# One decoder layer on one core: the front of the kernel rebuilt around the conditioning vector, constant products ahead of it, two groups in plain fp32, next weights prepared early

## The chip, the cores and the metric

The kernel runs on one core of one Trainium2 chip. The time is device time in microseconds of one execution; the time before is the median of three runs. The profile is one further execution with the hardware profiler on.

## What is computed

One conditioned layer over 256 tokens of width 2048, in fp32. Only the beginning matters here:

```
mod = silu(c) @ w_ada + b_ada          # c: one vector of 2048; six parts of 2048
shift1, scale1, ... = split(mod, 6)
h   = rms_norm(x, g_norm1) * (1 + scale1) + shift1
p   = h @ w_in                         # 2048 x 12288, then retention, HGRN2, gates
```

Everything behind `p` (two recurrent branches, two output projections, a gated feed-forward of width 5632 with a short convolution, the final norm) is untouched in its arithmetic.

## The kernel before

**Products.** A weight piece arrives by DMA as `raw`. ScalarE copies it to `wh`, a float32r tile (`upper`, L169), and VectorE subtracts to get the remainder `wl` (`rest`, L174). Activations are split into hi and lo in the same way. A product is then three float32r matmuls, hi·wh, lo·wh and hi·wl: L214, L215, L218 in `mm_cols`, and L198, L199, L203 in `mm_rows`. `raw` has 12 buffers, `wh` and `wl` 4 each, so a piece is prepared only when an earlier one has been used.

**Modulation.** `x` lies transposed (`xT`, four tiles of four 128-row blocks). Block k of `h` needs a scale column and a shift column: each is a dot product of silu(c), spread over all partitions in `sc`, with 128 rows of `w_ada`. `ada_dot` does it on VectorE, as two instructions of 1024 and 1025 columns per column vector (L458), so four per block. The norm needs 1/rms per token: `norm_x` squares the four tiles of `xT` and adds on VectorE; `token_rstd` sums over partitions with a column of ones on TensorE (L335), takes the square root on ScalarE (`rq`, L344), the reciprocal on VectorE (L345), and spreads the result with the identity (L349). `times` multiplies a block of `xT` by it (L448), `modulated` applies scale and shift (L382, L384, L386) and subtracts for lo (L387).

**The front.** `constants` brings `c` as two rows on one partition and spreads it with four matmuls against one row of ones (L296); ScalarE takes the Silu out of PSUM into `sc` (L368, L374). Then blocks k = 0 and 1 are multiplied with the first four column groups of `w_in` (`FIRST = 4`, groups 0 to 3, in PSUM).

**Behind the front.** A loop visits the groups 0 to 11 in turn, and lets each catch up with the blocks that are modulated by then: `have = min(KT, 2 + int((work - LAG) / ADA_EVERY))`, where `work` counts blocks times groups. A visited group other than 0 and 1 leaves its PSUM tile to `take`: the first time ScalarE copies it (`p<-pg`, L828), later VectorE adds it (L830).

**What sets the order.** In the front, instructions that go through `pin` keep the order in which they are written, engine by engine. Behind it a scheduler at build time chooses. Either way each engine works through one fixed list: an instruction that waits holds up what stands behind it on its engine. SyncE issues the weight DMAs (L158), ScalarE's queue the small ones of the start.

Of the kernel before, what the change touches and what calls it, by code (L numbers as in the profile page):

```python
# [12 lines left out]
F32 = mybir.dt.float32  # L13
# [22 lines left out]
LAG = 1  # L36
# [21 lines left out]
class Kernel:  # L58
    def __init__(self, ctx, tc, a):
# [12 lines left out]
        self.ordered = True  # L72

# [145 lines left out]

    def mm_wide(self, ps, items, first, last, pair):  # L220
# [54 lines left out]
    def constants(self):  # L275
# [13 lines left out]
        rows = [self.blk([1, GW], name="crow") for _ in range(2)]  # L289
        for u, row in enumerate(rows):  # L290
            nc.scalar.dma_start(out=row, in_=a["c"][:, u * GW : (u + 1) * GW])
        self.small_loads(nc.scalar, ("ident", "gn1"))
        for u in range(4):
            at = slice(u * G, (u + 1) * G)
            ps = self.po()
            nc.tensor.matmul(ps, lhsT=self.ones[0:1, :], rhs=rows[u // 2][:, u % 2 * G : (u % 2 + 1) * G], start=True, stop=True)  # L296
            self.silu.append((self.sc[:, at], ps))
# [29 lines left out]
    def token_rstd(self, parts):  # L327


        nc = self.nc  # L330
        ps = self.po()[:, :NT]
        for i, z in enumerate(parts):
            for t in range(NT):

                nc.tensor.matmul(  # L335
                    ps[:, t : t + 1],
                    lhsT=z[:, t * P : (t + 1) * P],
                    rhs=self.ones[:, 0:1],
                    start=i == t == 0,
                    stop=i == len(parts) - 1,  # L340
                    skip_group_check=True,
                )
        q = self.small([P, NT], name="rq")
        nc.scalar.activation(q, ps, AF.Sqrt, bias=self.eps1, scale=1.0 / D)  # L344
# [3 lines left out]
        for t in range(NT):  # L348
            nc.tensor.matmul(ps[:, t * P : (t + 1) * P], lhsT=q[:, t : t + 1].to_broadcast([P, P]), rhs=self.ident, start=True, stop=True)  # L349
# [7 lines left out]
    def norm_x(self):  # L357
# [3 lines left out]
        parts = []  # L361
        for i, x in enumerate(self.xT):
            z = self.blk([P, 4, T], name="sq")
            if i == 0:
                self.pin(nc.vector.tensor_tensor(z, x, x, ALU.mult))
            else:
                if i < 3:
                    self.pin(nc.scalar.activation(*self.silu.pop(0), AF.Silu))  # L368
                self.pin(nc.scalar.activation(z, x, AF.Square))
            self.pin(nc.vector.tensor_tensor(z[:, :2, :], z[:, :2, :], z[:, 2:, :], ALU.add))  # L370
            self.pin(nc.vector.tensor_tensor(z[:, 0, :], z[:, 0, :], z[:, 1, :], ALU.add))
            parts.append(z[:, 0, :])
        for part in self.silu:
            self.pin(nc.scalar.activation(*part, AF.Silu))  # L374
        self.sqrt_table()
        return parts

    def modulated(self, dst, x, k, sc, sh):
# [4 lines left out]
        if k == 0:  # L383
            self.pin(self.nc.vector.tensor_scalar(h, x, sc[:, k : k + 1], sh[:, k : k + 1], ALU.mult, ALU.add))  # L384
        else:
            self.pin(act(h, x, AF.Identity, bias=sh[:, k : k + 1], scale=sc[:, k : k + 1]))  # L386
# [65 lines left out]
    def ada_dot(self, src):  # L452

        nc = self.nc
        part = self.small([P, 2], name="dot", bufs=6)
        for u, w in enumerate((GW, D + 1 - GW)):
            raw = self.load(src[:, u * GW : u * GW + w], 1, w)
            dot = self.pin(nc.vector.scalar_tensor_tensor(raw[:, 0, :], raw[:, 0, :], 1.0, self.sc[:, u * GW : u * GW + w], ALU.mult, ALU.mult, accum_out=part[:, u : u + 1]))  # L458
# [5 lines left out]
    def scale_shift(self, name, k, sc, sh, gn):  # L464
# [5 lines left out]
        self.pin(act(sc[:, kk], gn[:, kk], AF.Identity, bias=gn[:, kk], scale=sc[:, kk]))  # L470
        part = yield from self.ada_dot(self.a[name][k, 1])
# [322 lines left out]
    def run(self):  # L794
# [38 lines left out]
        ada = [ada1(k) for k in range(KT)]  # L833
        for _ in range(3):
            next(ada[0])
        rx = self.token_rstd(parts)
        rx_sb = c.tile([P, T], F32, name="rx_sb")
        ps = [self.po2(), self.po2(), self.pg(), self.pg()][:FIRST]
        for k in range(2):
            for i in range(4 if k else 1):  # L840
                if k and i == 1:
                    self.times(k, 1, rx)
                next(ada[k])
            if k == 0:
                self.times(k, 1, rx)

            ahead = 2 * k
            uppers = [self.upper(a["wa"][g][:, k : k + 1, :], 1, G) for g in range(ahead + 1)]
            rests = [self.rest(z) for z in uppers[:ahead]]
            for _ in ada[k]:  # L850
                pass
            for g in range(FIRST):
                if g >= ahead:
                    rests.append(self.rest(uppers[g] if g < len(uppers) else self.upper(a["wa"][g][:, k : k + 1, :], 1, G)))
                wh, wl = rests[g]
# [436 lines left out]
```

## Time and profile before

| what | us |
|---|---|
| median of three runs | 1511.31 (1510.82 to 1512.48) |
| the profiled execution | 1511.24 |
| its span, first to last instruction | 1509.5 |

Lines of the profile name engines PE (TensorE matmul), PEld (its weight loads), DVE (VectorE), ACT (ScalarE), SP (SyncE); a q behind a name is the engine's instruction queue. In the timeline a row has start, time, engine, line, operation, output<-inputs, shape, count, and in brackets how long the engine had been idle and what ended that. The time of a row with a count runs from the first start to the last end. Instructions of one engine overlap a little, so that the distance between two starts (the pitch) is often shorter than the time of one. fp32 products show two records each, float32r products one.

### The profile page before, as it was taken

Reading aid. Unit: us, or ns where it says so; the run is one execution under the profiler, and the core shown is the slowest. Engines: PE = TensorE matmul, PEld = TensorE weight load, DVE = VectorE, ACT = ScalarE, POOL = GpSimd, SP = SyncE. Lnnn points to the kernel's source line nnn. Section 1 sums busy time; section 2 is a strip of 40 time slices with the busy share of each in tenths; the row PEclk is TensorE's granted clock in tenths of the full one; section 3 lists DMA queues with packets and bytes.
Section 4 is the critical chain, followed back from the end, with each engine's and each line's share of the span. In section 5 each row is a group of like instructions: output and inputs, shape, how many; then the busy total and the mean of one; then the engine's idle time right before and its main releaser. Section 6 shows DMA issues by size and latency. Waiting matters only on the chain.

```text
span 1509.5 us, 22703 instructions
## 1 busy us (share of the span) xinstructions
PE 1493.7 (99%) x8466; PEld 1275.5 (84%) x8466; DVE 1211.9 (80%) x1647; ACT 841.7 (56%) x1210; POOL 4.0 (0%) x8
## 2 busy tenths in 40 slices
PE   8999999999999999999999999999999999999997
PEld 6889899888888888888888888888888888888886
DVE  7899997998999877898977778777777769455784
ACT  6745456767775644455466555555555658344342
POOL 0000000000000000000000000000000000000000
PEclk9999999999999999999999999999999999999999
DMA  9999997777887899989847777777777666667651
GB/s 373 376 347 336 321 320 257 265 248 274 281 278 262 285 302 326 318 290 361 298 132 242 229 233 230 230 231 238 229 239 231 216 193 204 197 206 212 183 171 56
DMA packets 110994, 385.71 MB, mean 256 GB/s; under 512 B 12802, under 2 KB 13346, under 8 KB 110884
## 3 DMA queue, kind: packets, MB, share of 16 engines
q1 hardware_dynamic: 110016, 383.14, 76.7%
q8 instruction: 66, 1.08, 0.3%
q10 hardware_dynamic: 868, 1.13, 0.2%
q14 instruction: 44, 0.36, 0.1%
HBM read 382.11 MB, written 2.11 MB: 255 GB/s over the span
## 4 chain that ended last, share of the span: by engine, by line
PE 93%; DVE 3%; ACT 1%; issue 1%; DMA 1%; SPq 0%; DVEq 0%; ACTq 0%
PE pg L198 13%; PE pg L203 13%; PE pg L199 13%; PE po L1125 11%; PE pg L1125 10%; PE po L1127 5%; PE pg L1127 5%; PE pg L225 4%; PE po L198 3%; PE po L203 3%; PE po L199 3%; PE pg L228 2%; DVE wl L174 1%; DVE raw L458 1%; PE po L218 1%
## 5 line engine op out<-in xcount | busy, mean ns | idle before, releaser
L174 DVE TENSOR_TENSOR wl<-raw,wh 128x1024 fp32r<-128x1024 f32 (+1 forms) x536 | 633.1, 1191 | 233.6 <-ACT wh L169 230.6
L169 ACT ACTIVATE wh<-raw 128x1024 fp32r<-128x1024 f32 (+1 forms) x536 | 547.9, 1033 | 482.5 <-PE pg L199 167.0
L458 DVE SCALAR_TENSOR_TENSOR raw<-raw,sc 128x1024 f32<-128x1024 f32 x192 | 233.8, 1222 | 0.1
L1125 PE MATMUL po<-h2T,wh 128*128 128x512 f32 x704 | 221.1, 395 | 0.0
L1125 PE MATMUL pg<-h2T,wh 128*128 128x512 f32 x688 | 216.4, 396 | 0.0
L198 PE MATMUL pg<-wh,hT 128*128 128x512 f32 x512 | 202.1, 395 | 0.9 <-DVE p L830 0.6
L199 PE MATMUL pg<-wh,hT 128*128 128x512 f32 x512 | 199.8, 390 | 0.0
L1127 PEld LDWEIGHTS po<-h2T,wl 128*128 128x128 f32 x704 | 132.3, 188 | 31.3
L1127 PEld LDWEIGHTS pg<-h2T,wl 128*128 128x128 f32 x688 | 129.2, 188 | 31.0 <-DVE wl L174 0.5
L203 PE MATMUL pg<-wl,hT 128*128 128x512 f32 x512 | 138.4, 390 | 0.1
L1127 PE MATMUL po<-h2T,wl 128*128 128x256 f32 x704 | 138.3, 278 | 0.0
L1127 PE MATMUL pg<-h2T,wl 128*128 128x256 f32 x688 | 135.3, 278 | 0.1
L198 PEld LDWEIGHTS pg<-wh,hT 128*128 128x128 f32 x512 | 96.1, 188 | 21.3 <-ACT f L579 1.0
L203 PEld LDWEIGHTS pg<-wl,hT 128*128 128x128 f32 x512 | 96.0, 188 | 20.6 <-DVE wl L174 0.4
L199 PEld LDWEIGHTS pg<-wh,hT 128*128 128x128 f32 x512 | 96.2, 188 | 19.6 <-DVE hT L387 0.3
L1125 PEld LDWEIGHTS po<-h2T,wh 128*128 128x128 f32 x704 | 107.2, 189 | 0.0
L1125 PEld LDWEIGHTS pg<-h2T,wh 128*128 128x128 f32 x688 | 104.7, 189 | 0.0
L199 PE MATMUL pg<-wh,gs 128*128 128x512 f32 x176 | 68.6, 390 | 0.0
L198 PE MATMUL pg<-wh,gs 128*128 128x512 f32 x176 | 68.5, 389 | 0.0
L198 PE MATMUL po<-wh,gs 128*128 128x512 f32 x176 | 68.5, 389 | 0.0
L199 PE MATMUL po<-wh,gs 128*128 128x512 f32 x176 | 68.5, 389 | 0.0
L225 PE MATMUL pg<-hT,wh 128*128 128x512 f32 x256 | 65.1, 396 | 0.2 <-DVE p L247 0.2
(255 smaller groups left out, 2023.3 us busy)
## 6 DMA issues: line engine op xcount, KB each, us to landing
raw<-in_wup SPq DMA_DIRECT2D x176, 512.0 KB, 4.5
raw<-in_wdown SPq DMA_DIRECT2D x88, 512.0 KB, 4.2
raw<-in_wa SPq DMA_DIRECT2D x80, 512.0 KB, 5.7
raw<-in_ada SPq DMA_DIRECT2D x64, 512.5 KB, 5.4
raw<-in_ada SPq DMA_DIRECT2D x64, 512.0 KB, 5.5
raw<-in_wab SPq DMA_DIRECT2D x64, 512.0 KB, 5.0
raw<-in_gate SPq DMA_DIRECT2D x32, 512.5 KB, 4.3
raw<-in_wk SPq DMA_DIRECT2D x32, 512.0 KB, 5.1
```

The lines of the kernel that those rows point to most:

```text
L169: self.pin(self.nc.scalar.activation(wh, raw, AF.Copy))
L174: self.last = self.nc.vector.tensor_tensor(wl, raw, wh.bitcast(F32), ALU.subtract)
L198: nc.tensor.matmul(ps[t], lhsT=act[:, hi], rhs=wh, start=first and i == 0, stop=False)
L199: nc.tensor.matmul(ps[t], lhsT=act[:, lo], rhs=wh, start=False, stop=False)
L203: nc.tensor.matmul(ps[t], lhsT=act[:, hi], rhs=wl, start=False, stop=last and i == len(items) - 1)
L218: nc.tensor.matmul(outs[j], lhsT=wl[:, cs[j]], rhs=act[:, :T], start=False, stop=last and i == len(items) - 1, skip_group_check=True)
L225: nc.tensor.matmul(ps[z], lhsT=wh[:, z * P : (z + 1) * P], rhs=act, start=first and i == 0, stop=False)
L228: nc.tensor.matmul(ps[z][:, :T], lhsT=wl[:, z * P : (z + 1) * P], rhs=act[:, :T], start=False, stop=last and i == len(items) - 1)
L458: dot = self.pin(nc.vector.scalar_tensor_tensor(raw[:, 0, :], raw[:, 0, :], 1.0, self.sc[:, u * GW : u * GW + w], ALU.mult, ALU.mult, accu ...
L1125: self.pin(nc.tensor.matmul(ps[j + z], lhsT=wh[:, cs[z]], rhs=act, start=kt == 0, stop=False, skip_group_check=bool(begun)))
L1127: nc.tensor.matmul(ps[j + z][:, :T], lhsT=wl[:, cs[z]], rhs=act[:, :T], start=False, stop=kt == KT - 1, skip_group_check=bool(begun))
```

## The change

1. `c` comes as 16 rows of 128 and, behind the identity, on ScalarE's queue. TensorE transposes it (L320 of the new file), ScalarE takes one Silu of 128x16 (`col`, L323) and loads the square-root table at once. `spread` makes the four pieces of `sc` with four 128x128 products each (`col` broadcast, against the identity, L334); ScalarE copies them out (L410, L422).
2. `idle(n)` issues n products of constant ones, which nobody reads (L242): nine at the start, one behind the transpose, two and nine in `token_rstd`.
3. The fourth tile of `xT` is squared half by ScalarE, half by VectorE, and its four parts go to TensorE unadded: the sums over partitions become 14 products (L370) in place of 8.
4. For blocks 0 and 1 the second shift dot is cut into 512 and 513 columns. The modulation starts with scale and the first part of the shift (`begun`, L891), and VectorE adds the other two (`summed`, L882).
5. For block 0, groups 0 and 1 are multiplied in plain fp32 straight from `raw` (`mm_plain`, L225): no `wh`, no `wl`. For block 1, groups 0 and 1 go through `mm_apart` (L236), all hi·wh, then lo·wh, then hi·wl.
6. The `wh` and `wl` of group 4's first two blocks are made in the pinned part (`self.early`), ahead of block 2's dots. `LAG` goes from 1 to 2.

The numbers of float32r products behind the front stay the same; VectorE has three more `take` additions (40 for 37).

```diff
-LAG = 1
+LAG = 2
@@ Kernel
+    def mm_plain(self, ps, w, h):
+        for j in range(4):
+            out = ps[j // 2][:, j % 2 * T : (j % 2 + 1) * T]
+            self.pin(self.nc.tensor.matmul(out, lhsT=w[:, j * P : (j + 1) * P], rhs=h, start=j % 2 == 0, stop=False, skip_group_check=True))
+
+    def mm_apart(self, pss, pieces, act):
...
+        for pick, cols in ((0, slice(0, T)), (0, slice(T, 2 * T)), (1, slice(0, T))):
+            for i in n:
+                for j in range(4):
...
+    def idle(self, n):
+        ps = self.pg()[0]
+        for _ in range(n):
+            self.pin(self.nc.tensor.matmul(ps[:, :P], lhsT=self.ones, rhs=self.ones, start=True, stop=True))
@@ products
-        for step in self.pieces(src[:, k0 : k0 + kts, :], kts, gain):
+        early, self.early = self.early, None
+        for step in early or self.pieces(src[:, k0 : k0 + kts, :], kts, gain):
@@ constants
-        rows = [self.blk([1, GW], name="crow") for _ in range(2)]
-        for u, row in enumerate(rows):
-            nc.scalar.dma_start(out=row, in_=a["c"][:, u * GW : (u + 1) * GW])
-        self.small_loads(nc.scalar, ("ident", "gn1"))
-        for u in range(4):
...
-            nc.tensor.matmul(ps, lhsT=self.ones[0:1, :], rhs=rows[u // 2][:, u % 2 * G : (u % 2 + 1) * G], start=True, stop=True)
+        self.small_loads(nc.scalar, ("ident",))
+        row = self.s1([KT, P], name="crow")
+        self.pin(nc.scalar.dma_start(out=row, in_=a["c"]))
+        self.small_loads(nc.scalar, ("gn1",))
+        self.idle(9)
+        ps = self.po()[:, :KT]
+        self.pin(nc.tensor.transpose(ps, row, self.ident[:KT, :KT]))
+        self.idle(1)
+        col = self.small([P, KT], name="col", bufs=1)
+        self.pin(nc.scalar.activation(col, ps, AF.Silu))
+        self.sqrt_table()
+        self.col = col
+        for u in range(2):
+            self.spread(u)
+
+    def spread(self, u):
+        ps = self.po()
+        for i in range(4):
+            k = 4 * u + i
+            self.pin(self.nc.tensor.matmul(ps[:, i * P : (i + 1) * P], lhsT=self.col[:, k : k + 1].to_broadcast([P, P]), rhs=self.ident, start=True, stop=True))
+        self.silu.append((self.sc[:, u * G : (u + 1) * G], ps))
@@ token_rstd
+        self.idle(2)
         q = self.small([P, NT], name="rq")
...
+        self.idle(9)
@@ norm_x
+            elif i < 3:
+                self.pin(nc.scalar.activation(z, x, AF.Square))
+                self.pin(nc.scalar.activation(*self.silu.pop(0), AF.Copy))
             else:
-                if i < 3:
-                    self.pin(nc.scalar.activation(*self.silu.pop(0), AF.Silu))
-                self.pin(nc.scalar.activation(z, x, AF.Square))
+                self.pin(nc.scalar.activation(z[:, :2, :], x[:, :2, :], AF.Square))
+                self.pin(nc.vector.tensor_tensor(z[:, 2:, :], x[:, 2:, :], x[:, 2:, :], ALU.mult))
...
+            self.sums(ps, [z[:, j, :] for j in range(1 if i < 3 else 4)], i == 0, i == 3)
+            if i == 0:
+                for u in (2, 3):
+                    self.spread(u)
@@ scale_shift
+        if fine:
+            yield from self.ada_dot(self.a[name][k, 1], (0, GW, GW + G, D + 1))
+            return
@@ run
+        def summed(dst, z, part):
+            self.pin(nc.vector.tensor_scalar(dst, z, part[:, 1:2], part[:, 2:3], ALU.add, ALU.add))
...
+        def begun(k):
+            z = self.s1([P, T], name="z")
+            self.pin(nc.scalar.activation(z, self.xT[0][:, k, :], AF.Identity, bias=self.part[:, 0:1], scale=s1[:, k : k + 1]))
+            return z
...
+        next(gen)
+        self.times(0, 1, rx)
+        self.pin(nc.scalar.activation(rx_sb, rx, AF.Copy))
+        z = begun(0)
...
+        summed(h, z, self.part)
...
+        plain = [self.load(a["wa"][g][:, 0:1, :], 1, G) for g in range(RESIDENT)]
...
+        for g in range(RESIDENT):
+            self.mm_plain(ps[g], plain[g][:, 0, :], h)
...
+        summed(hi, z, self.part)
+        h = self.s1([P, T], name="h")
+        summed(h, z, self.part)
+        self.pin(nc.vector.tensor_tensor(lo, h, hi.bitcast(F32), ALU.subtract))
+        rests = [self.rest(z) for z in uppers]
+        self.mm_apart([ps[g] for g in range(RESIDENT)], rests, act(1))
...
+        self.early = list(self.pieces(a["wa"][FIRST][:, 0:2, :], 2))
...
-        work = 2 * FIRST
+        work = sum(done)
```

Three places in the engines' lists, as they stand in the two programs. Names carry the number of the buffer and of the tile.

TensorE at the start, before: the four spreading products (L296), the sums over partitions (L335), the spreading of 1/rms (L349).

```order
L296 MATMUL po_3_87<-crow_1_79,ones_69 128x512
L296 MATMUL po_4_89<-crow_1_79,ones_69 128x512
L296 MATMUL po_5_91<-crow_2_80,ones_69 128x512
L296 MATMUL po_6_93<-crow_2_80,ones_69 128x512
L335 MATMUL po_33_154<-ones_69,sq_11_103 128x1 x2
L335 MATMUL po_33_154<-ones_69,sq_12_107 128x1 x2
L335 MATMUL po_33_154<-ones_69,sq_13_112 128x1 x2
L335 MATMUL po_33_154<-ones_69,sq_14_117 128x1 x2
L349 MATMUL po_35_166<-ident_83,rq_34_163 128x128 x2
```

And now, from behind the transpose:

```order
L242 MATMUL pg_4_97<-ones_69 128x128
L334 MATMUL po_7_103<-ident_79,col_5_99 128x128 x4
L334 MATMUL po_8_108<-ident_79,col_5_99 128x128 x4
L370 MATMUL po_13_121<-ones_69,sq_14_122 128x1 x2
L334 MATMUL po_15_128<-ident_79,col_5_99 128x128 x4
L334 MATMUL po_16_133<-ident_79,col_5_99 128x128 x4
L370 MATMUL po_13_121<-ones_69,sq_17_138 128x1 x2
L370 MATMUL po_13_121<-ones_69,sq_18_145 128x1 x2
L370 MATMUL po_13_121<-ones_69,sq_19_152 128x1 x8
L242 MATMUL pg_35_188<-ones_69 128x128 x2
L390 MATMUL po_37_194<-ident_79,rq_36_191 128x128 x2
L242 MATMUL pg_38_197<-ones_69 128x128 x9
```

The sums of the later tiles now stand behind the spreading products, and eight of them belong to the last tile.

VectorE at the dots of block 0 (`dot` tiles), before: the reciprocal (L345) stands behind the third dot.

```order
L458 SCALAR_TENSOR_TENSOR raw_29_142,dot_28_141<-raw_29_142,sc_77 128x1024
L458 SCALAR_TENSOR_TENSOR raw_30_145,dot_28_141<-raw_30_145,sc_77 128x1025
L458 SCALAR_TENSOR_TENSOR raw_32_151,dot_31_150<-raw_32_151,sc_77 128x1024
L345 RECIPROCAL rq_34_163<-rq_34_163 128x2
L458 SCALAR_TENSOR_TENSOR raw_42_176,dot_31_150<-raw_42_176,sc_77 128x1025
L448 TENSOR_TENSOR xT_7_95<-xT_7_95,po_35_166 128x256
```

And now:

```order
L413 TENSOR_TENSOR sq_19_152<-xT_12_116 128x512
L502 SCALAR_TENSOR_TENSOR raw_33_182,dot3_32_181<-raw_33_182,sc_77 128x1024
L502 SCALAR_TENSOR_TENSOR raw_34_185,dot3_32_181<-raw_34_185,sc_77 128x1025
L386 RECIPROCAL rq_36_191<-rq_36_191 128x2
L502 SCALAR_TENSOR_TENSOR raw_40_211,dot4_39_210<-raw_40_211,sc_77 128x1024
L492 TENSOR_TENSOR xT_9_113<-xT_9_113,po_37_194 128x256
L502 SCALAR_TENSOR_TENSOR raw_42_218,dot4_39_210<-raw_42_218,sc_77 128x512
L502 SCALAR_TENSOR_TENSOR raw_43_221,dot4_39_210<-raw_43_221,sc_77 128x513
L882 TENSOR_SCALAR h_44_224<-z_41_216,dot4_39_210 128x256
```

The reciprocal has moved up by one dot: the third dot now waits behind it.

ScalarE where the front ends, before. `pg_40` and `pg_41` are groups 2 and 3, `pg_71` is group 4, `wh_73`, `wh_78` and `wh_84` are the weights of groups 4, 5 and 6.

```order
L169 ACTIVATE wh_73_366<-raw_72_364 128x1024
L469 ACTIVATE s1_125<-dot_68_354 128x1
L470 ACTIVATE s1_125<-gn1_85,s1_125 128x1
L828 ACTIVATE p_18_131<-pg_40_174 128x1024
L169 ACTIVATE wh_78_392<-raw_77_390 128x1024
L828 ACTIVATE p_19_132<-pg_41_175 128x1024
L828 ACTIVATE p_20_133<-pg_71_363 128x1024
L472 ACTIVATE t1_126<-dot_74_384 128x1
L169 ACTIVATE wh_84_421<-raw_83_419 128x1024
```

And now. `pg_56` and `pg_60` are groups 2 and 3, `pg_80` is group 4, `wh_76`, `wh_85` and `wh_89` are the weights of groups 4, 5 and 6.

```order
L170 ACTIVATE wh_76_383<-raw_75_381 128x1024
L875 ACTIVATE p_22_171<-pg_56_258 128x1024
L875 ACTIVATE p_23_172<-pg_60_278 128x1024
L513 ACTIVATE s1_165<-dot3_77_388 128x1
L514 ACTIVATE s1_165<-gn1_83,s1_165 128x1
L875 ACTIVATE p_24_173<-pg_80_397 128x1024
L170 ACTIVATE wh_85_420<-raw_84_418 128x1024
L170 ACTIVATE wh_89_443<-raw_88_441 128x1024
```

Group 5's weights stood ahead of the copy of group 4's sums; now they stand behind it.

More of the change, by code (lines that the diff above doesn't have):

```diff
@@ L72, in __init__ @@
         self.ordered = True
+        self.early = None
     def blk(self, shape, dtype=F32, name="b"):
@@ L360, in norm_x @@
         self.xT = self.load_x()
[L361 removed]
+        ps = self.po()[:, :NT]
         for i, x in enumerate(self.xT):
@@ L836, in run @@
+        ada = [None, None, *(ada1(k) for k in range(2, KT))]
+        gen = first(0)
+        for _ in range(2):
+            next(gen)
         rx = self.token_rstd(parts)
         rx_sb = c.tile([P, T], F32, name="rx_sb")
[L838 to L855, printed above, removed]
-                if k == g == 0:
-                    self.pin(nc.scalar.activation(rx_sb, rx, AF.Copy))
-                mms[g](ps[g], [(act(k), wh[:, 0, :], wl[:, 0, :])], k == 0, k == 1 and g >= RESIDENT)
@@ new lines, in run @@
+        self.pin(nc.vector.tensor_tensor(lo, h, hi.bitcast(F32), ALU.subtract))
+        rests = [self.rest(z) for z in uppers]
+        self.times(1, 1, rx_sb)
+        gen = first(1)
+        for g in range(RESIDENT):
+            self.mm_plain(ps[g], plain[g][:, 0, :], h)
+        for g in range(RESIDENT, FIRST):
+            ps[g] = self.pg()
+            wh, wl = rests[g - RESIDENT]
+            mms[g](ps[g], [(act(0), wh[:, 0, :], wl[:, 0, :])], True, False)
+            for _ in range(2):
+                next(gen)
@@ L859, in run @@
+        for g in range(RESIDENT, FIRST):
+            wh, wl = self.rest(self.upper(a["wa"][g][:, 1:2, :], 1, G))
+            mms[g](ps[g], [(act(1), wh[:, 0, :], wl[:, 0, :])], False, True)
+        self.early = list(self.pieces(a["wa"][FIRST][:, 0:2, :], 2))
         for _ in range(2):
@@ L1267, in _arrays @@
     out["gate2"] = adaT[5]
+    out["ident"] = np.eye(P, dtype=np.float32)
     out.update(_tables())
```

89 lines of the change are left out of this document (53 added, 36 removed).

## The prediction

> **What bounds the kernel now.** I read the page first, then TensorE's waits, then the timeline of the front.
>
> ```profile
> span 1509.5 us, 22703 instructions
> PE 1493.7 (99%) x8466; PEld 1275.5 (84%) x8466; DVE 1211.9 (80%) x1647; ACT 841.7 (56%) x1210; POOL 4.0 (0%) x8
> ```
>
> TensorE is busy for 99% of the span, so only time in which it has nothing useful can be won. Its waits over the whole run (engine, line, what it waited for: total, times, longest) lie almost all in the front:
>
> ```profile
> PE po L296 <- DMA crow<-in_c: 2.5, 1, 2.5
> PE po L214 <- ACT hT L382: 1.7, 2, 1.2
> PE po L349 <- DVE rq L345: 1.6, 1, 1.6
> ...
> PE po L215 <- DVE hT L387: 0.2, 1, 0.2
> ```
>
> The timeline of the front, in time order:
>
> ```profile
> 2.46 7.16 PE L296 MATMUL po<-crow,ones 1*128 1x512 f32 x8 [2.46 <-DMA crow<-in_c]
> 9.55 3.57 PE L335 MATMUL po<-ones,sq 128*128 128x1 f32 x16
> 10.90 1.22 DVE L458 SCALAR_TENSOR_TENSOR raw<-raw,sc 128x1024 f32<-128x1024 f32 x1
> 14.48 0.16 DVE L345 RECIPROCAL rq<-rq 128x2 f32<-128x2 f32 x1
> 14.70 1.22 PE L349 MATMUL po<-ident,rq 128*128 128x128 f32 x4 [1.58 <-DVE rq L345]
> 17.11 0.80 PE L214 MATMUL po<-hT,wh 128*128 128x256 f32 x2 [1.20 <-ACT hT L382]
> 21.79 0.41 PE L215 MATMUL pg<-hT,wh 128*128 128x256 f32 x1
> 22.00 0.41 PE L214 MATMUL pg<-hT,wh 128*128 128x256 f32 x1
> 24.40 0.28 PE L214 MATMUL pg<-hT,wh 128*128 128x256 f32 x1
> 24.52 0.28 PE L215 MATMUL pg<-hT,wh 128*128 128x256 f32 x1
> 26.00 0.74 PE L214 MATMUL po<-hT,wh 128*128 128x256 f32 x4 [0.48 <-ACT hT L382]
> 32.71 0.50 PE L198 MATMUL pg<-wh,hT 128*128 128x512 f32 x1 [0.22 <-ACT p L828]
> 20.00:25.00 5.00, 5.00 (x35) 5.00 (x33) 5.00 (x10) 2.34 (x5) 0.00 (x0) 1.00 1.04 400
> ```
>
> Real products begin at 17.11. The same 256-column product has a pitch of 0.21 at 22.00 and 0.12 at 24.40: TensorE runs at half rate until then, although the last row (a five-us stretch: busy time of PE, PEld, DVE, ACT, POOL, then granted clock, DMA share, GB/s) grants 1.00; I read the rate off the pitches. The seven us of L296, one row of ones, and the 3.57 of L335, one column each, did not raise it. Block 1 begins at 26.00, group 4 at 32.71. What the front is worth is when group 4, and what follows it, can start.
>
> **The dots of block 0.** Durations of ScalarE, VectorE and the small DMAs:
>
> ```profile
> 0.73 0.78 ACTq L291 DMA_DIRECT2D crow<-in_c  x2
> ident<-in_ident ACTq DMA_DIRECT2D x1, 64.0 KB, 4.7
> 2.45 1.28 ACT L368 ACT_TABLE_LOAD   x1 [2.45 <-issue]
> 6.03 1.06 ACT L369 ACTIVATE sq<-xT 128x1024 f32<-128x1024 f32 x1 [0.90 <-DMA xT<-in_xT]
> 9.71 1.07 ACT L374 ACTIVATE sc<-po 128x512 f32<-128x512 f32 x2
> 12.09 0.20 ACT L355 ACTIVATE warm<-eps 128x1 f32<-128x1 f32 x1
> 13.16 0.26 ACT L344 ACTIVATE rq<-po,eps 128x2 f32<-128x2 f32 x1 [0.87 <-PE po L335]
> 16.97 0.36 ACT L857 ACTIVATE rx_sb<-po 128x256 f32<-128x256 f32 x1
> 5.76 0.69 DVE L370 TENSOR_TENSOR sq<-sq 128x512 f32<-128x512 f32 x1
> 15.96 0.42 DVE L448 TENSOR_TENSOR xT<-xT,po 128x256 f32<-128x256 f32 x1
> 17.44 2.49 DVE L174 TENSOR_TENSOR wl<-raw,wh 128x512 fp32r<-128x512 f32 x4
> 21.32 1.22 DVE L458 SCALAR_TENSOR_TENSOR raw<-raw,sc 128x1025 f32<-128x1025 f32 x1
> 22.47 1.22 DVE L458 SCALAR_TENSOR_TENSOR raw<-raw,sc 128x1024 f32<-128x1024 f32 x1
> ```
>
> The second row is a DMA's time from issue to landing. The identity takes the first place on ScalarE's queue, 0.73; with its 4.7 it lands at 5.4. The first nine constant products need two records of 0.21 each at the slow rate, 3.8 us from about 1.0, and hold nothing up. Transpose and Silu: 0.3 each by the small ScalarE row, so `col` stands at 6.0. ScalarE then does what it did later before: table 1.28, warm 0.20, to 7.5; squares 1.06, copy 0.53, squares 1.06, to 10.15. VectorE adds twice (0.69 and 0.42), squares half a tile (0.69) and begins the first dot at about 11.6, with the overlaps of neighbours taken off; before it was 10.90. So the dots begin later, not earlier: +0.7 us.
>
> Dots follow at a pitch of 1.15: the second ends at 13.9. Now the reciprocal stands ahead of the third. It needs the eight sums of the last tile, ready from 11.9: 16 records, at 3.57 / 16 = 0.22 at the slow rate and half of it at the full. No row shows constant products raising the rate; the nearest are L214 to L218, full of columns, which did after 5.3 us (17.11 to 22.4). The constant and spreading products are as full (128 columns) and stand from 1.0 to about 11 with one gap near 5, so I take the full rate: 1.8 us, out at 14.0 with a record's length, root 0.26, reciprocal done at 14.45. VectorE waits 0.4 there, and behind it stand the dots that everything else waits for.
>
> [...]
>
> From 14.45: dot 1.15, times 0.34, two half dots 0.6 each, 0.1 for the accumulator, `summed` 0.42: `h` at 17.7 where 17.11 was. ScalarE's copy and the start of block 1 follow on VectorE: copy 0.36, lo 0.42, two `wl` of 0.6 (2.49 less 0.69 over three), times 0.34, together with semaphores to 20.05. Three dots 3.45, two halves 1.2, 0.1 and `summed` 0.42: hi of block 1 at 25.2, against 26.00. The cut of the second shift dot, the additions and the missing `wl` of groups 0 and 1 buy this 0.8 in spite of the late start. TensorE is ready for it: eight plain products of two 256-column records, 16 at 0.21, 3.4 us, and 24 at 0.12, 2.9, from 17.7 to 24.0. The last nine constant products (1.9 at full rate behind L390) end before 17.7 and cost nothing; the cover is VectorE's dots, and at half rate it is gone.
>
> Block 1 takes 48 products at 0.12, 5.8, and without the 0.48, 0.2 and 0.22 of waits: group 4 starts at 31.0 instead of 32.71, 1.7 us won.
>
> **Group 5.** What a first visit does to ScalarE is in the trace:
>
> ```profile
> 34.66 1.07 PE L203 MATMUL pg<-wl,hT 128*128 128x512 f32 x4
> 35.56 0.39 PE L198 MATMUL pg<-wh,hT 128*128 128x512 f32 x1
> 35.76 1.03 ACT L828 ACTIVATE p<-pg 128x1024 f32<-128x1024 f32 x1 [1.14 <-PE pg L203]
> 36.69 0.28 ACT L472 ACTIVATE t<-dot 128x1 f32<-128x1 f32 x1
> 36.87 1.05 ACT L169 ACTIVATE wh<-raw 128x1024 fp32r<-128x1024 f32 x1
> ```
>
> This is the copy of group 4: ScalarE sat idle for 1.14 until group 4 was through, 0.2 behind the start of group 5, and only then made `wh` of group 6, in time. In the changed list this copy stands ahead of group 5's own `wh`. Group 4: 12 products at 0.227 (34.66 to 35.56 is four), 2.7, to 33.7. Copy from 33.9, next instruction 0.93 later (35.76 to 36.69), `wh` 1.05, handover and restart 0.15: group 5 starts at 36.0, against 35.56. TensorE stands for 2.3, and VectorE's `wl` and take queue behind. The 1.7 are gone, and 0.45 more. Group 7's `wh` stands behind the copy of group 5 in the same way and comes 0.2 late, because with LAG 2 group 6 has two blocks to hide it, not three.
>
> **LAG.** It asks for block 2 one group later, a cover for dots that now start earlier relative to the groups; I cost that at nothing. But it makes three more additions of a whole group on VectorE. There the next bound lies:
>
> ```profile
> 100.00:130.00 30.00, 29.93 (x171) 26.23 (x170) 29.89 (x47) 14.80 (x23) 0.95 (x1) 1.00 0.96 334
> 119.08 0.76 PEld L203 LDWEIGHTS pg<-wl,hT 128*128 128x128 f32 x4 [0.38 <-DVE wl L174]
> 110.66 1.13 DVE p L830
> ```
>
> VectorE is busy for 29.89 of 30 us (third busy time), and once TensorE waited 0.38 for it. (The last row is from the chain of waits.) I counted, in the two lists, VectorE's work from an addition that needs a finished group to each later `wl`, against TensorE's work in between, with the pitches above and 1.13 an addition: before, the worst stretch has 23.1 of VectorE against 22.6, and 0.38 was seen; now 80.5 against 79.4. So 0.6 us more. Ends: nothing, if the copy's stall has let VectorE get ahead; 1.5 if it also counts the 0.4 idle of ScalarE there.
>
> Other parts: the plain groups hold their `raw` until TensorE is through, about 20 and 21.5, in place of `wl`; SyncE's queue stands behind them, with over three us of issued loads ahead, so nothing. One DMA less for `c`, two more for cut dots: nothing, same bytes.
>
> Sum: +0.45 +0.2 +0.6 = +1.2 on the profiled 1511.24, which is 0.07 below the median: **1512.4**.
>
> **Rivals.**
>
> *The front's gain is kept.* If group 5's `wh` is not held by the copy, or the stall covers what would be lost later, 2.3 us come back: 1510.1; with the first dot at 10.90 and no wait at the reciprocal, 1.1 less, 1509.0. For it: 1.14 us of idle ScalarE is harmless in the row above. Against: the order is fixed in the list.
>
> *Nothing changes.* VectorE is the bound of the stretch to 130 us and not the front: a TensorE that arrives 0.5 early or late finds the same wait. Then 1511.3. For it: 29.89 of 30. Against: VectorE's own work starts with the front too.
>
> *Slower: the sums run slow.* The point is 11.9: if the records of the sums still have a pitch of 0.2 there, sums take 1.8 more, the reciprocal and the third dot with them, the nine constant products behind L390 take 3.8 from 17 and stand ahead of the plain products, which start at 21 at half rate until about 22.4, and end at 28 where block 1 was ready at 27. Group 4 at 33.7, group 5 at 38.7: 2.7 us on top, 1515.1. For it: L296 and L335, ten us of TensorE without effect on the rate. Against: those are thin products, these full ones.
>
> **How the numbers follow.** Forecast 0.6, gain kept 0.15, nothing 0.12, slow sums 0.13. About 0.2%, 3.0 us, is what a measurement of this kernel tells from no change. Faster than 1508.3 needs the first rival at its best and an unforeseen gain in VectorE's stretch: 0.05. Slower than 1514.3 is the third rival and a little of the forecast, where the VectorE term is at its end: 0.13. The rest, 0.82, is within. The forecast's own range is 1510.5 to 1514.0 (0.9 of the front either way, 0 to 1.5 in VectorE's stretch); the range 1509.2 to 1515.0 takes in the kept gain and all but the end of the slow sums.
>
> **What would show it.** First dot between 11.0 and 12.0; pitch of the spreading records 0.11 by 9; a wait of VectorE at the reciprocal; first plain product near 17.7; block 1's first hi product near 25.2; group 4 near 31.0; then a wait of TensorE of over 2 us on ScalarE's `wh` ahead of group 5, the copy of group 4 just before it; a VectorE wait near 105 or 165. The prediction is wrong if group 5 starts before 35, if the sums end after 15, or if waits behind 170 us, which I left as they are, change by over a microsecond.

## The result, and the profile after

The change makes the kernel slower: 1537.95 us median (1537.04 to 1540.26, four runs) beside 1511.13 (1510.82 to 1512.48, four runs). The ratio is 1.0178 [1.016, 1.0196]. Forecast were 1512.4 and a range up to 1515.0.

From the page of the changed kernel: the span, the engines' busy times (us, share, instructions), and three groups of products (line, output<-inputs, shape, count, then busy us, mean ns of one, idle before).

```profile
span 1535.0 us, 22857 instructions
PE 1519.8 (99%) x8537; PEld 1282.7 (84%) x8537; DVE 1215.0 (79%) x1654; ACT 843.4 (55%) x1211; POOL 4.0 (0%) x8
...
L204 PE MATMUL pg<-wl,hT 128*128 128x512 f32 x512 | 142.0, 395 | 0.9 <-DVE wl L175 0.9
L1213 PE MATMUL po<-h2T,wl 128*128 128x256 f32 x704 | 140.5, 281 | 0.0
...
L252 PE MATMUL pg<-hT,wl 128*128 128x256 f32 x256 | 35.2, 280 | 0.0
```

The same groups before, where `mm_rows`' third line is L203, the up projection's L1127, and `mm_wide`'s L228:

```profile
L203 PE MATMUL pg<-wl,hT 128*128 128x512 f32 x512 | 138.4, 390 | 0.1
L1127 PE MATMUL po<-h2T,wl 128*128 128x256 f32 x704 | 138.3, 278 | 0.0
L228 PE MATMUL pg<-hT,wl 128*128 128x256 f32 x256 | 35.7, 282 | 0.0
```

VectorE and ScalarE work as long as before (1211.9 and 841.7 us there). TensorE is busy 26.1 us longer, with as many products behind the front as before: a product of 512 columns takes 395 ns for 390, one of 256 takes 281 for 278 in one place and 280 for 282 in another. Products overlap, so the better figure is their pitch: a stretch divided by the products that start in it. Two stretches that hold nothing but products, of the kernel before (busy time of TensorE, count, granted clock, DMA share, GB/s). The first is the up projection, one product of 512 columns to one of 256; the second the down projection, 512 columns only.

```profile
800.00:1240.00 440.00, 440.00 (x2528) 1.00 0.73 227
1300.00:1460.00 160.00, 160.00 (x708) 1.00 0.66 198
```

And of the kernel after:

```profile
800.00:1240.00 440.00, 439.89 (x2502) 1.00 0.73 228
1300.00:1460.00 160.00, 160.00 (x688) 1.00 0.66 196
```

160 us over 708 is 226.0 ns, over 688 it is 232.6: +6.6 a product, at a granted clock of 1.00 and nearly the same DMA load. In the up projection the mean of the two kinds goes from 174.1 to 175.9. An estimate from these pitches: about 3,360 products of the first sort at 6 to 6.6 ns make 20 to 22 us, 2,784 of the up projection at 1.8 make 5, some 1,000 of 256 columns out of `hT` win 2 back: 23 to 25. The front adds 0.9 (below), and the span grew by 25.5.

The front came out nearly as forecast. Its timeline after:

```profile
6.36 2.05 PE L334 MATMUL po<-ident,col 128*128 128x128 f32 x16
11.53 2.36 PE L370 MATMUL po<-ones,sq 128*128 128x1 f32 x20 [0.54 <-DVE sq L416]
11.90 1.22 DVE L502 SCALAR_TENSOR_TENSOR raw<-raw,sc 128x1024 f32<-128x1024 f32 x1
13.93 0.26 ACT L385 ACTIVATE rq<-po,eps 128x2 f32<-128x2 f32 x1 [1.76 <-PE po L370]
15.34 3.52 PE L242 MATMUL pg<-ones 128*128 128x128 f32 x18
18.69 3.62 PE L225 MATMUL po<-h,raw 128*128 128x256 f32 x16
25.72 2.12 PE L236 MATMUL po<-hT,wh 128*128 128x256 f32 x16 [0.53 <-DVE hT L882]
31.43 0.40 PE L199 MATMUL pg<-wh,hT 128*128 128x512 f32 x1
31.66 0.40 PE L200 MATMUL pg<-wh,hT 128*128 128x512 f32 x1
33.31 1.09 PE L204 MATMUL pg<-wl,hT 128*128 128x512 f32 x4
34.44 1.02 ACT L875 ACTIVATE p<-pg 128x1024 f32<-128x1024 f32 x1 [0.89 <-PE pg L204]
35.35 2.00 ACT L170 ACTIVATE wh<-raw 128x1024 fp32r<-128x1024 f32 x2
36.45 0.50 PE L199 MATMUL pg<-wh,hT 128*128 128x512 f32 x1 [2.06 <-ACT wh L170]
14.00:18.00 4.00, 3.91 (x21) 0.59 1.06 414
```

The last row is a stretch of four us, in which the granted clock was 0.59. Group 5 starts at 36.45, where it was 35.56: the front costs 0.9 us. What the forecast did not have is the rest of the run.

What could change the pitch of products that nobody touched? One step of the change moves `crow` from a large activation tile (`blk`, tag k4) to a small one (`s1`, tag k1). Tags get their place in SBUF in the order in which the program first uses them. So the seven small tiles (7168 bytes), `col` and `warm` (160 bytes) now come ahead of the large activation tiles, which begin at byte 107072 of a partition instead of 99744. `raw`, `wh` and `wl` lie where they lay. Before, activation and weight tiles began at the same place within 4096 bytes (`wh` begins at byte 66976, and 99744 - 66976 is 8 times 4096). The same edit order swaps the two kinds of PSUM tiles: the constant products take a `pg` tile ahead of the first `po`.

### The profile page after: what moved, and what is told of

It is laid out like the page before. It is cut to its first block, busy times and chain, and to the rows that moved or that the text cites. A ratio compares the mean times of both kernels' runs of the same rounds, so it can differ in the third digit from the quotient of the medians.

```text
span 1535.0 us, 22857 instructions
## 1 busy us (share of the span) xinstructions
PE 1519.8 (99%) x8537; PEld 1282.7 (84%) x8537; DVE 1215.0 (79%) x1654; ACT 843.4 (55%) x1211; POOL 4.0 (0%) x8
## 4 chain that ended last, share of the span: by engine, by line
PE 94%; DVE 3%; ACT 2%; issue 1%; DMA 0%; DVEq 0%; ACTq 0%
PE pg L199 13%; PE pg L204 13%; PE pg L200 13%; PE po L1211 11%; PE pg L1211 10%; PE po L1213 5%; PE pg L1213 5%; PE pg L249 4%; PE po L200 3%; PE po L199 3%; PE po L204 3%; PE pg L252 2%; PE pg L216 1%; PE pg L215 1%; PE pg L219 1%; PE po L219 1%
## 5 line engine op out<-in xcount | busy, mean ns | idle before, releaser
L502 DVE SCALAR_TENSOR_TENSOR raw<-raw,sc 128x1024 f32<-128x1024 f32 (+2 forms) x194 | 234.1, 1210 | 0.0
L199 PE MATMUL pg<-wh,hT 128*128 128x512 f32 x512 | 204.9, 400 | 2.5 <-ACT wh L170 2.1
L200 PE MATMUL pg<-wh,hT 128*128 128x512 f32 x512 | 202.2, 395 | 0.0
L204 PE MATMUL pg<-wl,hT 128*128 128x512 f32 x512 | 142.0, 395 | 0.9 <-DVE wl L175 0.9
```

Of the source, the lines that this page charges most:

```text
L199: nc.tensor.matmul(ps[t], lhsT=act[:, hi], rhs=wh, start=first and i == 0, stop=False)
L200: nc.tensor.matmul(ps[t], lhsT=act[:, lo], rhs=wh, start=False, stop=False)
L204: nc.tensor.matmul(ps[t], lhsT=act[:, hi], rhs=wl, start=False, stop=last and i == len(items) - 1)
```

## Experiments: where the 25 us come from

Three theories: P, the place of the activation tiles against the weight tiles; Q, the order in PSUM; R, something in the front that lowers TensorE's rate for good.

**32 bytes (e1_sb32).** The kernel before, with one line ahead of the first `blk`:

```diff
+        nc.vector.memset(self.small([P, 8], name="pad", bufs=1), 1.0)
```

> The kernel before, with one unused tile of 32 bytes ahead of the activation tiles, so that they lie 32 bytes further in SBUF, while the weights wh and wl stay. Theory P (the pitch of the products depends on where the activation tiles lie against the weight tiles): the 512-column pitch rises from 227 to over 230 ns and the time to 1520 to 1540 us. Theory Q (it is the order of the PSUM tiles, which the changed kernel swaps) and theory R (TensorE's rate is lowered for good by the constant products): 1511, pitch 227.

1528.26 us (1527.57 to 1537.6, four runs), ratio 1.0122 [1.0093, 1.0151]. The same two stretches:

```profile
800.00:1240.00 440.00, 439.89 (x2490) 1.00 0.71 227
1300.00:1460.00 160.00, 160.00 (x687) 1.00 0.62 196
```

A tile of 32 bytes that is written once and never read costs over 16 us: the pitch of the down projection is 232.9. Theory P is shown. One thing stays open: the execution with the profile took 1537.6, the other three 1527.6 to 1528.4. The 9 us between them is about what the up projection costs more in the profile than before (176.7 for 174.1 over 2,784 products is 7 us), so its pitch may differ from execution to execution at this offset; this profile also has one stretch of 3.4 us at half clock, from 27.37, worth up to 1.7 us. The other three have no profile, so this stays a guess.

**PSUM order, put into the kernel before (e2_psum) and taken out of the kernel after (e4_after_psum).** One constant product into a `pg` tile ahead of all else; and the first constant products into a `po` tile.

> The kernel before, with one constant product into a pg tile first, so that pg takes PSUM banks 0 to 3 and po 4 to 7, as in the changed kernel. Theory Q: over 1530. Theories P and R: 1511 to 1512.

> The changed kernel, with the first of the constant products into a po tile, so that po takes PSUM banks 0 to 3 and pg 4 to 7, as before. Theory Q: 1512 to 1514. Theories P and R: 1537 to 1540.

1511.9 (ten runs, ratio 1.0001 [0.9992, 1.0011]) and 1538.73 (four runs, ratio 1.0179 [1.0164, 1.0194]). Q falls both ways.

**The change with the activation tiles at their old place (e3_after_sb).**

```diff
-        row = self.s1([KT, P], name="crow")
+        row = self.blk([KT, P], name="crow")
```

> The changed kernel, with the row of c in a tile of the activation pool, as before, so that the activation tiles begin at the byte at which they did. Theory P: the pitch is back at 227, and the time is that of the front alone, 1511.5 to 1513.5 (group 5 starts 0.9 us late in the trace, 36.45 for 35.56). Theories Q and R: 1537 to 1540.

1515.25 us (1513.64 to 1517.18, ten runs), ratio 1.0023 [1.0013, 1.0032], and in the profile:

```profile
800.00:1240.00 440.00, 440.00 (x2528) 1.00 0.71 228
1300.00:1460.00 160.00, 160.00 (x708) 1.00 0.63 200
```

Both counts are those of before to the last product. So 22.7 of the 26.8 us are one word in one line, and R falls: all of the new front is still there. The time is above the 1511.5 to 1513.5 that was expected. What is left, +3.6 us by the medians, is not the tiles' place but the rest of the change, and the next section takes it apart.

**Which offsets count (e5_sb64, e6_all32, e12_k1first).** The kernel before with 64 bytes ahead of the activation tiles; with 32 bytes ahead of the weight tiles, so that both move together; and with the seven small tiles ahead of the large ones, 7168 bytes, as in the change but without the 160 of `col` and `warm`.

```diff
# e5
+        nc.vector.memset(self.small([P, 16], name="pad", bufs=1), 1.0)
# e6
+        nc.vector.memset(c.tile([P, 8], F32, name="pad"), 1.0)
# e12
+        nc.vector.memset(self.s1([P, 8], name="pad"), 1.0)
```

> The kernel before with an unused tile of 64 bytes a partition ahead of the activation tiles: they begin at byte 99808 instead of 99744, the weight tiles stay. The 32-byte shift gave 1528.3. Theory P-far (the offset of the activation tiles to the weight tiles counts, whatever it is): slower again, 1520 to 1540, pitch of the 512-column products 232 to 235 ns. Rival P-unit (only the place within a unit of 64 bytes counts, activations and weights in the same half of it or not): 1511.6, pitch 227 ns. The trace of before shows no other offset, so even chances.

> The kernel before with an unused tile of 32 bytes a partition ahead of the weight tiles and the activation tiles: both move by 32 bytes, their offset to each other stays. If the offset counts (P-far and P-unit): 1511.6 and a pitch of 227 ns for 512 columns. Rival P-place (the place of a tile by itself counts, a start that is a multiple of 64 bytes is worse): both operands now begin at a multiple of 64, so at least the 1528.3 of the 32-byte shift, pitch 233 ns or more.

> The kernel before, in which the small activation tiles (1024 bytes each, seven of them) are allocated ahead of the large ones, as in the change, but without the 160 bytes of `col` and `warm` that lie between them there: the large activation tiles move by 7168 bytes, a multiple of 1024, where the change moved them by 7328. Every instruction but one memset stands where it stood. Theory P-any (any new offset to the weight tiles slows the products): 1520 to 1540, pitch of the 512-column products 232 to 235 ns. Rival P-low (only the part of the offset below 512 bytes counts, which is what the columns of one weight load take): 1511.6, pitch 227.

64 bytes: 1525.69 us (ratio 1.0092 [1.0079, 1.0106]). Both by 32: 1512.13 (1.0002 [0.9993, 1.0012]). 7168 bytes: 1511.62 (1.0 [0.999, 1.0009]). The down projection in the three, in this order:

```profile
1300.00:1460.00 160.00, 160.00 (x687) 1.00 0.62 193
```

```profile
1300.00:1460.00 160.00, 160.00 (x708) 1.00 0.64 200
```

```profile
1300.00:1460.00 160.00, 160.00 (x707) 1.00 0.64 200
```

The first is as theory P-far has it, the second and the third as the offset and P-low have it. It is not the place of a tile, and not whether it starts at a multiple of 64 bytes (in the second run the activations, `wh` and `wl` all do, before none of them): it is the offset between activations and weights. Of the change's 7328 bytes, 7168 by themselves cost nothing (1511.62), so it is the 160 of `col` and `warm` that cost. That 512 bytes are the unit, as the expectation had it, is not shown: 7168 is 7 times 1024 too, and no run tried 512.

**A better offset for one stage (e10_up64).** With 64 bytes the up projection alone was faster:

```profile
800.00:1240.00 440.00, 439.87 (x2550) 1.00 0.73 231
```

172.5 ns for 174.1. Products with `wh` and with `wl` stand there in pairs; a `wh` product with another behind it had a pitch of 227.4 for 232.9, all `wh` products together 229.0 for 233.1. So in the kernel before, `wh` of the up projection was put 64 bytes lower in its slot, all else left:

```diff
+        at = self.turns % 4 * 2 * G + (0 if up else 16)
+        self.turns += 1
+        wh = self.whs[:, at : at + m * w].rearrange("p (m w) -> p m w", m=m)
-        wh = self.wp.tile([P, m, w], F32R, name=f"wh_{self.n}", tag="wh", bufs=4)
```

> The kernel before, in which wh of the up projection alone (the 712 products of 512 columns out of h2T) lies 64 bytes lower in its slot; everything else keeps its offset to the activations. With all tiles 64 bytes apart those products had a pitch of 227.4 ns instead of 232.9, the others rose. Theory: the pitch is set by the offset of the two operands of that stage alone, so 712 times 5.5 ns = 3.9 us are won: 1507.8, and the 256-column products with wl stay at 114.8. Rival: the pitch hangs on the operand loaded for the next product too, so the wl products beside them rise by 2 ns (1.4 us): 1509.2. Third: nothing, 1511.8.

1512.45 us (1511.75 to 1513.45, eleven runs), ratio 1.0007 [0.9999, 1.0016]. Nothing was won:

```profile
800.00:1240.00 440.00, 440.00 (x2522) 1.00 0.72 227
```

174.5 ns, where before had 174.1. The starts within it show why. All products with `wh` went from a mean of 233.1 to 232.0, and those with `wl`, whose own tiles had not moved, from 115.2 to 117.2. The `wl` products rose by 2 ns as the rival said, and `wh` kept only 1.1 of the 4.1. The up projection has 1,392 products of each kind (704 and 688 in the lists by line), not the 712 of the expectation, so these means come to 1.5 us won and 2.8 lost.

The offset of a product's own two operands therefore does not set its pitch alone: where one `wl` product stands ahead of another, neither of which had moved, the pitch still rose from 114.6 to 116.7. Here the operands of the products around it counted too, and no run separates which. By what way they slow a product was not shown; the mean of a weight load by itself in the up projection is 188 to 189 ns before the change and 187 to 189 after it.

## Experiments: the front with the tiles in place

TensorE's waits in the change with its tiles at the old place (waiting line, what it waited for: total, times, longest):

```profile
PE pg L199 <- ACT wh L170: 2.1, 1, 2.1
...
PE pg L204 <- DVE wl L175: 1.0, 1, 1.0
PE pg L199 <- DVE p L877: 1.0, 2, 0.5
```

And in the kernel before, the waits for `p` alone:

```profile
PE pg L198 <- DVE p L830: 0.6, 1, 0.6
```

The first is the forecast wait ahead of group 5. The second lies at 103.8, in the stretch in which VectorE is the bound (busy for 29.89 of the 30 us from 100 to 130 before); before, TensorE lost 0.1 to such waits. The third are two waits for additions at 282.5 and 290.1; before has one, at 275.8.

**Group 5's parts early too (e7_early2); LAG 1 (e8_lag1).** Both start from e3_after_sb.

```diff
# e7
-        self.early = list(self.pieces(a["wa"][FIRST][:, 0:2, :], 2))
+        for g in (FIRST, FIRST + 1):
+            self.early.append(list(self.pieces(a["wa"][g][:, 0:2, :], 2)))
# e8
-LAG = 2
+LAG = 1
```

> The change with the activation tiles at their old place (1515.25), and the parts of group 5's first weights made ahead of group 4's copy too, so that ScalarE's list has them in time. Theory W (the wait of 2.1 us for wh ahead of group 5 is what the front loses): the wait goes and the time falls by about 2 us, to 1513.2. Rival V (VectorE bounds the stretch to 120 us): the wait moves there, TensorE waits for wl or p instead, time 1515 within 0.5.

> The change with the activation tiles at their old place (1515.25), and block 2 asked for one group earlier (LAG 1), as before the change. Theory W: the wait of 2.1 us ahead of group 5 stays, and 1.6 us of waits for VectorE between 100 and 120 us go, since whole-group additions fall away: 1513.7. Rival: group 6 or 7 now waits for block 2's dots at about 40 us, over 1 us, and nothing is won: 1515 to 1516.

e7: 1515.48 us (1513.43 to 1516.7, eleven runs), nothing won, but not as the rival had it. The wait moved by one group:

```profile
34.15 0.39 PE L199 MATMUL pg<-wh,hT 128*128 128x512 f32 x1
37.07 1.02 ACT L875 ACTIVATE p<-pg 128x1024 f32<-128x1024 f32 x1
37.99 1.05 ACT L170 ACTIVATE wh<-raw 128x1024 fp32r<-128x1024 f32 x1
39.09 0.69 PE L199 MATMUL pg<-wh,hT 128*128 128x512 f32 x1 [2.06 <-ACT wh L170]
39.58 0.63 PE L200 MATMUL pg<-wh,hT 128*128 128x512 f32 x1
38.00:42.00 4.00, 2.91 (x7) 0.65 1.02 402
```

Group 5 now starts at 34.15 without a wait, and group 6, at 39.09, stands 2.06 us behind the copy of group 5. The copy of a group is the cost as long as it stands ahead of the next group's `wh` in ScalarE's list; making more ahead of it only moves the place. The last row adds something: behind this wait the granted clock falls to half (0.50 from 40 to 42), and eight products run at a pitch of 0.43, where e3_after_sb has 0.23.

e8: 1514.21 us (1512.92 to 1515.22, eleven runs), ratio 1.0016 [1.0007, 1.0024]. A microsecond less than 1515.25, which is not clear of noise: the ranges and the intervals of the two ratios overlap. In the profiles the wait for `wl` fell from 1.0 to 0.6 and the waits for `p` from 1.0 to the 0.6 of before, 0.7 in all, where 1.6 had been expected. Nothing waits for block 2's dots, and the 2.1 stayed.

**The copy behind the weights (e9_wh5_first).** As e8, and on ScalarE's list group 5's `wh` stands ahead of the copy of group 4. In the code `take` of a group is put off until the next group has its first pieces, and both are pinned:

```diff
+                    self.force = done[g] == 0 and g == FIRST + 1
+                    ps_g = self.products(mms[g], self.pg(), a["wa"][g], act, done[g], m)
+                    if done[g] == 0 and m == 2 and g + 1 < len(ATT):
+                        self.late = partial(take, g, ps_g, True)
+                    else:
+                        take(g, ps_g, done[g] == 0)
```

> As the run with LAG 1 (1514.21; activation tiles at their old place), with one thing changed on ScalarE: the copy of group 4's sums stands behind group 5's wh instead of ahead of it. Theory W (the copy is what TensorE waits for ahead of group 5): in the run of the change with its tiles at the old place group 4's products end at 33.6, the two small instructions ahead of wh end at 33.2, wh takes 1.05: group 5 starts at about 34.4, the wait falls from 2.1 to 0.8, and the time by 1.3, to 1512.9; by up to 1.7 more in those executions in which the granted clock fell to half behind that wait. Rival V (VectorE's stretch gives it back): the wait for wl or p near 105 to 165 us grows by as much, 1514.2 within 0.5.

1511.97 us (1511.35 to 1512.48, eleven runs), ratio 1.0002 [0.9993, 1.0011].

```profile
34.19 1.07 PE L209 MATMUL pg<-wl,hT 128*128 128x512 f32 x4
34.26 1.04 ACT L173 ACTIVATE wh<-raw 128x1024 fp32r<-128x1024 f32 x1
35.30 1.03 ACT L883 ACTIVATE p<-pg 128x1024 f32<-128x1024 f32 x1
35.36 0.50 PE L204 MATMUL pg<-wh,hT 128*128 128x512 f32 x1
```

`wh` first, the copy behind it, and the wait is a quarter of a microsecond. That is 2.2 us less than e8, or 1.9 when each is set against the runs of before beside it, and the two ranges do not touch. The wait itself fell by 1.8, not by 1.3. So theory W holds, and rival V does not: the wait for `wl` at 102 to 104 us is 0.64 in both runs and did not grow.

The kernel now is as fast as before the change and no faster. Group 5 starts at 35.36 for 35.56, and the run stays 0.1 to 0.3 ahead of before up to 100 us. The wait for `wl` at 101.75, which before does not have, turns this into 0.8 behind; e8 loses the same microsecond there. The wait for an addition at 276.6, 0.6, is that of before.

**Without the constant products (e11_no_const).** e3_after_sb with `idle` empty.

> The change with the activation tiles at their old place (1515.25), without its 30 constant products of 128 columns. Theory C (they raise TensorE's rate early): the sums and the spread of the reciprocal have pitches of over 0.2 us, the plain products run at half rate until about 22, group 4 starts at 33.5 instead of 30.8 and the time is 2.7 longer, 1518. Rival D (the dots set the front, and a clock that is not raised early is not taken away again at 13 to 18 us): within 1 us of 1515.25.

1517.26 us (1515.69 to 1517.59, five runs), ratio 1.0035 [1.0021, 1.0049], by the medians 2.0 more than with them. The ranges of the two overlap, so the profiles have to decide. The change has 21 such products (42 records), not the 30 of the expectation.

```profile
12.87 2.74 PE L368 MATMUL po<-ones,sq 128*128 128x1 f32 x24
16.25 0.68 PE L388 MATMUL po<-ident,rq 128*128 128x128 f32 x4 [0.65 <-DVE rq L384]
19.36 6.58 PE L225 MATMUL po<-h,raw 128*128 128x256 f32 x16 [2.43 <-DVE h L880]
34.40 0.40 PE L199 MATMUL pg<-wh,hT 128*128 128x512 f32 x1
18.00:22.00 4.00, 2.64 (x6) 0.54 1.03 397
```

Theory C holds in the result, but only in part by the way that it named. With the spreading products alone the rate is up too, only later, at 11.5: the sums (24 records in 2.74) and the four records of the reciprocal (0.68, as in e3_after_sb) run at the full rate. But the first half of the spreading products runs slow (16 records in 3.79), the sums come later with them, and the plain products begin at 19.36, where e3_after_sb has 17.05. TensorE has stood for 2.43 just before, the granted clock is halved from 18.4 to 25.2 (0.50 from 20 to 24), and the plain products take 6.58, where e3_after_sb took 3.72. Group 4 starts at 34.40 instead of 30.83. Those 3.6 us are the distance of the two profiled executions, 1517.26 and 1513.64.

## Why the prediction was wrong

**The step that failed** is the one that costs "other parts" at nothing and takes every product from the trace of before: "Group 4: 12 products at 0.227". Group 4 in the changed kernel already runs slower: from its second product to its twelfth it takes 2.35 us, where it took 2.30 before and takes 2.29 in e3_after_sb. The line of the diff that did it, `row = self.s1(...)`, was read as a matter of 16 rows for one, not as one that moves every activation tile. That moved the offset between activations and weights by 7328 bytes, and the 512-column pitch from 226.0 to 232.6 ns. The price is 22.7 us, by e3_after_sb; no rival had it. The last sentence of what would show it named a change of the waits behind 170 us; the waits there moved by less than half a microsecond in all, the products between them slowed down.

**The front's steps**, against the trace after:

- First dot 11.6: 11.90. Spreading products 0.11 by 9: 16 in 2.05, 0.128. Sums at the full rate, out at 14.0: `rq` at 13.93. The third rival, slow sums, did not come: the records of the constant products had a pitch of 0.21 up to 4.4 and of 0.11 from 4.6, so that the rate was up at 4.5, 3.4 us behind the first of them. It was up by 6.0 in five of the six profiles with these products, and only at 9.7 in e9_wh5_first.
- "The last nine constant products (1.9 at full rate behind L390) end before 17.7 and cost nothing": the rate fell to half between 14.73 and 18.15 (granted clock 0.50), they took 3.52, and the plain products began at 18.69, not 17.7. In e3_after_sb the rate stayed (granted clock 1.00 from 10 to 22), and they began at 17.05. The microsecond cost nothing all the same: TensorE still stood for 0.53 ahead of block 1, waiting for VectorE's `hi`. So the 0 was right, with less to spare than was thought.
- Block 1 at 25.2, group 4 at 31.0: 25.72 and 31.43. Of the half microsecond 0.3 is the later start of VectorE's dots.
- The copy of group 4 ahead of group 5's `wh`: right in place, cause and size, 2.06 us for 2.3; group 5 at 36.45 for 36.0. e9_wh5_first shows it by undoing it. Group 7 has no wait; that 0.2 was too much.
- VectorE's stretch, 0.6 with an end of 1.5: a wait for `wl` of 0.87 at 105.5, near where it was forecast, and no more than that in the changed kernel. The 0.38 that was read for before is the idle time of a weight load; the products themselves lost 0.1 there.

With the tiles in place the front's forecast can be held against a run. The prediction's 1512.4 is 2.9 under the 1515.25 of e3_after_sb, which lies just outside its range too. In that profile group 5 starts at 35.80, 0.24 behind before, where 0.45 was forecast. At the first product of the feed-forward the run is 2.1 behind before. That product in e3_after_sb, and in the kernel before:

```profile
769.48 0.95 PE L1190 MATMUL pg<-h2T,wh 128*128 128x256 f32 x6 [0.65 <-DVE h2T L474]
```

```profile
767.35 1.18 PE L1104 MATMUL pg<-h2T,wh 128*128 128x256 f32 x8 [0.65 <-DVE h2T L430]
```

So 1.9 us were lost between, where the prediction had 0.6 for VectorE and 0.2 for group 7. This term was too small; 1.3 of it are the longer waits for `wl` and `p` above. The profiled execution, 2.4 over before (1513.64 against 1511.24), is also the fastest of the ten; that the median lies another 1.6 higher may be the clock's doing, as the last section says, and is not shown.

## What to carry to other kernels

A change that allocates a small tile earlier, or a tile from another pool, moves everything that is allocated behind it (here by 7328 bytes). Compare the byte addresses of the two matmul operands before and after. Where a kernel has been tuned with one offset, keep it, or time the new one: here 7168 bytes more cost nothing (1511.62), 32 and 64 cost 16.6 and 13.9 us by the medians, 7328 cost 22.7. If the pitch of untouched products changes over the whole run with no new wait (here from 226.0 to 232.6 ns), look there first.

Making the next group's operand early did not help (e7_early2, 1515.48 for 1515.25) while the copy that frees the last group stood ahead of a later group's operand in the same engine's list; the wait of 2.06 us only moved by a group. What helped here is their order (e9_wh5_first, 1511.97 for the 1514.21 of e8_lag1).

## What the runs showed of the hardware

- **The pitch hangs on 32 bytes.** At equal clock (1.00), nearly equal DMA load (0.62 to 0.66) and, but for the changed kernel, instruction lists that are the same but for one memset, the 512-column products of the down projection ran at 226 or 233 ns by the offset of their operands in SBUF. 32, 64 and 7328 bytes (the changed kernel) were slow for these, 232.9, 232.9 and 232.6, 0 and 7168 fast, 226.0 and 226.3; the up projection was fastest at 64, 172.5 for the 174.1 of 0. Of these offsets the kernel before stood at a good one for most of its work.
- **Half a clock came in stretches of 3.4 us, or of twice that.** In the changed kernel the half-rate stretch in the front lasts from 14.73 to 18.15 (granted clock 0.50), 3.41 us. In the first 44 us of the other profiles those of e1_sb32, e4_after_psum and e7_early2 are 3.4 us long, those of e8_lag1 and e11_no_const 6.8, by the granted clock of stretches of two to four us. What starts one was not shown. In the 3.41 us ahead of the fall at 14.73 TensorE's records cover 3.11 us, most of them sums of one column. And of six profiles with the wait of 2.06 us, two fell to half behind it (e7_early2, and e4_after_psum below), four did not.

```profile
36.52 0.62 PE L199 MATMUL pg<-wh,hT 128*128 128x512 f32 x1 [2.06 <-ACT wh L170]
```

  Eight products at 0.43 instead of 0.23 are 1.6 us. The ten times of e3_after_sb lie at 1513.6 to 1514.2, 1515.2 to 1515.9 and 1517.1 to 1517.2, steps of 1.6; the eleven of e9_wh5_first, without the wait, lie within 1.1. That each step is one such stretch is a reading that no run shows: one stretch takes 0.001 off the mean granted clock of an execution, by an estimate (half of 3.41 in 1512), and the means of the ten, 0.996 to 0.998, do not follow the times (0.998 at 1513.64 and at 1517.18).
